# Four more query tiles in the paired front, differential heads spread over one more unit, and a conditioning block in the last projection of a two-layer diffusion trunk

## Chip, cores, metric

One core of a Trainium2 chip runs the whole program in one launch. The metric is device time in microseconds, the median over several executions. Engines are named as in the profile: PE is TensorE (PEld its weight loads), DVE VectorE, ACT ScalarE, POOL GpSimd, SP the sync engine that issues most DMAs.

## What is computed

512 latent tokens and 128 context tokens, 640 columns in all, of width 2048 pass two layers: a norm with shift and scale from a condition vector, one combined input projection, mixers with gates, an output projection, and a gated residual. Layer 1, which the change is about, in the reference's words (cut):

```python
def odd_mixer(h, w_in, w_out, cqn, ckn, c_lam, c_on, dqn, dkn, lam_init, ctx=None, rope=None):
    cq, ck, cv, cg, dq, dk, dv, dg = split_cols(h @ w_in, ODD_SPLIT)
...
    o1 = attend(cq[:, 0][:, :, None], ck_all[:, 0], cv_all)[:, :, 0]
    o2 = attend(cq[:, 1][:, :, None], ck_all[:, 1], cv_all)[:, :, 0]
    o_c = rms_norm(o1 - lam.astype(o1.dtype) * o2, c_on) * (1.0 - lam_init)
    y_c = o_c.transpose(0, 2, 1, 3).reshape(b, t, C_W) * jax.nn.silu(cg)
    y_d = merge_heads(attend(q_d, dk_all, dv_all)) * jax.nn.silu(dg)
    return jnp.concatenate([y_c, y_d], axis=-1) @ w_out, new
```

Mixer C has four differential heads, each with two softmax maps over the same values, so each needs two query tiles (cq h and cq 4 + h). Mixer D has eight ordinary heads, handled as four pairs that share a softmax step. Latent queries read 256 cached context keys and 512 latent keys; context queries read 128.

The shift, scale and gate come from a product of the condition with a 2048 x 6144 matrix for each layer, cut into twelve conditioning blocks of 512 columns. Block 11 of layer 1 holds the last quarter of the gate, needed for output columns 12 to 15 of the last projection.

## The kernel before, in words

Everything is float32, with operands split into a high and a low part (split, L336: ScalarE writes the high part, VectorE the low one), and each product made of three matmuls (high x high, low x high, high x low). Columns are the 640 tokens, in two halves of 320. A projected tile is 128 output columns for all tokens.

There are two ways to project. run_tiles (L430) makes a tile directly, over 16 input blocks, quarter by quarter; its weight quarters are loaded five and split three ahead. run_pairs (L583) makes two tiles at once with a Winograd form of Strassen's scheme: products M1, M5, M6, M2, M7, M3, M4, each over eight input blocks and one half of the tokens, from sums of weights and of inputs that VectorE forms. Between half products it calls slot (L421), which moves the waiting work on: late softmax scalings, prep (generators for keys, queries, values), attn (the attention generators, paced in steps per slot), and a fill generator, by a credit per product that rests gives.

Layer 1 runs in three stages.

*Front* (L1736 to L1863): six gate tiles directly, then 16 pairs: gates, ten keys, four queries of mixer D, ten values. Their results go to DRAM scratch (gdram, kdram, qdram, vdram). Keys are normed, turned and transposed back by key_chain (L1765). The fill, fill1, is ada_in_psum (L222) for blocks 8 to 10: weights of a block come in 16 loads on POOL's queue, and VectorE adds each, times two scalars, onto rows in PSUM; ada_fold (L257) then sums over partitions with matmuls and transposes back.

*Attention* (L1865 to L1968): 14 tiles by run_tiles: the four first queries of each pair of mixer D, then two queries for each head of mixer C, then two gates. After a query tile, q_gen (L791) or, for one that comes back from DRAM, q_rider (L813) norms and turns it; head_rest (L1924) brings keys and values. The attention work goes between the matmuls of the tiles: 3.1 steps per quarter for the first five tiles, 1.75 after. pair_gen (L953) and diff_gen (L1645) go through five blocks of 128 queries, one unit each, in two steps: score, softmax, transposes of the probabilities (groups), the product with the values (weigh), for differential heads the norm and the transposed output (out), each some units behind the score. Block 11 is made here, by ada_in_rows (L244), on VectorE with loads on SP's queue; its remaining calls run before the first pair of heads is set going (first, L1914).

*Last projection* (project_out, L1352, through project, L1309): two lead tiles whose inputs come in as the last head ends, four single tiles beside which forms (L1249) makes the sums of inputs, then five pairs, with rows transposed and stored.

PSUM tiles: one bank pair S for scores (two of them in the attention stage), two banks T for everything transposed or weighted. Tiles of the SBUF name "xr" rotate through five places. The order of instructions on an engine is that of the program as a list scheduler has laid it out, so an instruction with operands not ready yet can stand behind later ones.

## Time and profile before

| | us |
|---|---|
| median of 3 runs | 2247.62 (2247.52 to 2248.9) |
| the profiled execution | 2246.84 |
| its span, first to last instruction | 2245.1 |
| six gate tiles and 16 front pairs of layer 1 end | 1598.8 |
| attention stage | 1598.8 to 2018.5 |
| last projection | 2018.5 to 2241 |

Times in the trace count from the first instruction. A row of the busy view has a stretch, its length, then busy time and instructions of PE, PEld, DVE, ACT and POOL, the granted TensorE clock, the DMA engines' share and GB/s. A row of a group has line, engine, operation, output and inputs, count, then busy time, mean ns of one, and the idle time ahead of them with what ended it. A wait row has who waited for whom, total us, times, and the longest. A matmul's shown length overlaps the next one's, so matmuls are counted by their number in a stretch.

### The profile page before, as it was taken

The numbers are of one execution on the slowest core, as the hardware profiler recorded it, in microseconds if no ns is written. First come the engines' busy times: TensorE is split into PE (matmuls) and PEld (weight loads), VectorE is DVE, ScalarE is ACT, GpSimd is POOL, SyncE is SP. The second block draws the span as 40 slices with busy tenths as digits, with TensorE's granted clock in tenths as the row PEclk, the third lists the DMA queues.
The fourth block names the chain that finished last, engine by engine and source line by source line (L and its number), as shares of the span: only waits on it lengthen the run. The fifth ranks groups of instructions, "written<-read, shape, count | busy, mean of one in ns | idle before, by whom it ended". The sixth has DMA issues, their size and how long they took to land.

```text
span 2245.1 us, 41142 instructions
## 1 busy us (share of the span) xinstructions
PE 2202.9 (98%) x15516; PEld 2126.6 (95%) x15516; DVE 1748.3 (78%) x3047; ACT 1135.5 (51%) x2443; POOL 253.3 (11%) x405
## 2 busy tenths in 40 slices
PE   7999999999999999999999999999989999999999
PEld 5889999999999999999999999999978999999999
DVE  5659898989888977878788878887686567776665
ACT  4334453535344445444654466545567766664343
POOL 3221001000100100000101012211101001111010
PEclk9999999999999999999999999999999999999999
DMA  9985556565454435844774434545542233357541
GB/s 355 339 289 176 164 167 209 174 200 167 141 158 121 145 103 180 244 141 123 231 235 150 146 99 126 162 134 159 179 148 84 69 98 109 92 163 238 170 132 45
DMA packets 381399, 368.47 MB, mean 164 GB/s; under 512 B 18946, under 2 KB 326624, under 8 KB 380688
## 3 DMA queue, kind: packets, MB, share of 16 engines
q1 hardware_dynamic: 359552, 288.97, 43.0%
q0 software_dynamic: 20784, 74.63, 9.4%
q8 instruction: 122, 2.00, 0.4%
q10 hardware_dynamic: 864, 2.23, 0.3%
q14 instruction: 77, 0.63, 0.1%
HBM read 312.41 MB, written 48.11 MB: 161 GB/s over the span
## 4 chain that ended last, share of the span: by engine, by line
PE 84%; DVE 4%; DMA 4%; issue 4%; ACT 3%; POOL 1%; SPq 0%; DVEq 0%; POOLq 0%; ACTq 0%
PE pq L676 12%; PE pq L677 12%; PE pq L678 12%; PE pa L373 5%; PE pa L374 5%; PE pa L375 5%; PE pb L375 5%; PE pb L373 5%; PE pb L374 5%; PE T L914 2%; PE S L926 2%; PE S L928 1%; PE S L927 1%; PE T L196 1%; PE T L706 1%
## 5 line engine op out<-in xcount | busy, mean ns | idle before, releaser
L337 ACT ACTIVATE wh<-raw 128x512 fp32r<-128x512 f32 (+1 forms) x352 | 210.7, 600 | 324.0 <-PE pb L374 198.7
L676 PE MATMUL pq<-h,wh 128*128 128x320 f32 x1152 | 358.0, 311 | 0.0
L677 PE MATMUL pq<-h,wh 128*128 128x320 f32 x1152 | 356.0, 309 | 0.0
L678 PE MATMUL pq<-h,wl 128*128 128x320 f32 x1152 | 355.7, 309 | 0.0
L373 PE MATMUL pa<-h,wh 128*128 128x320 f32 x944 | 300.1, 318 | 0.0
L375 PE MATMUL pa<-h,wl 128*128 128x320 f32 x944 | 293.5, 311 | 3.3 <-DVE wl L338 3.3
L373 PE MATMUL pb<-h,wh 128*128 128x320 f32 x944 | 295.6, 314 | 1.1 <-ACT h L337 0.9
L375 PE MATMUL pb<-h,wl 128*128 128x320 f32 x944 | 294.5, 312 | 1.0 <-DVE wl L338 1.0
L374 PE MATMUL pa<-h,wh 128*128 128x320 f32 x944 | 294.5, 312 | 0.4 <-DVE h L338 0.4
L374 PE MATMUL pb<-h,wh 128*128 128x320 f32 x944 | 293.7, 311 | 0.0
L338 DVE TENSOR_TENSOR wl<-raw,wh 128x512 fp32r<-128x512 f32 (+1 forms) x352 | 228.5, 650 | 81.1 <-ACT wh L337 75.4
L676 PE MATMUL pq<-T,wh 128*128 128x320 f32 x864 | 268.7, 311 | 0.0
L678 PE MATMUL pq<-T,wl 128*128 128x320 f32 x864 | 267.2, 309 | 0.3 <-DVE wl L338 0.3
L677 PE MATMUL pq<-T,wh 128*128 128x320 f32 x864 | 266.9, 309 | 0.0
L337 ACT ACTIVATE wh<-sx 128x512 fp32r<-128x512 f32 x216 | 135.9, 632 | 171.5 <-PE pq L677 114.0
L676 PEld LDWEIGHTS pq<-h,wh 128*128 128x128 f32 x1152 | 216.3, 188 | 1.2 <-issue 1.2
L677 PEld LDWEIGHTS pq<-h,wh 128*128 128x128 f32 x1152 | 216.4, 188 | 0.0
L678 PEld LDWEIGHTS pq<-h,wl 128*128 128x128 f32 x1152 | 216.3, 188 | 0.0
L291 DVE SCALAR_TENSOR_TENSOR acc<-adaw,sT,acc 128x1024 f32<-128x1024 f32 x150 | 189.5, 1277 | 0.0
L373 PEld LDWEIGHTS pa<-h,wh 128*128 128x128 f32 x944 | 177.7, 188 | 10.2 <-issue 9.3
L374 PEld LDWEIGHTS pa<-h,wh 128*128 128x128 f32 x944 | 177.7, 188 | 5.2 <-issue 4.5
L375 PEld LDWEIGHTS pa<-h,wl 128*128 128x128 f32 x944 | 177.6, 188 | 4.4 <-DVE wl L338 3.6
(416 smaller groups left out, 5007.5 us busy)
## 6 DMA issues: line engine op xcount, KB each, us to landing
adaw<-in_ada_w SPq DMA_DIRECT2D x80, 512.0 KB, 4.2
raw<-in_ev_w_in SPq DMA_DIRECT2D x130, 256.0 KB, 3.5
raw<-in_od_w_in SPq DMA_DIRECT2D x112, 256.0 KB, 3.4
w<-in_od_w_in SPq DMA_DIRECT2D x48, 512.0 KB, 4.2
ada<-in_ada_w SPq DMA_DIRECT2D x11, 2048.0 KB, 13.5
adaw<-in_ada_w POOLq DMA_DIRECT2D x59, 256.0 KB, 3.5
w<-in_ev_w_in SPq DMA_DIRECT2D x27, 512.0 KB, 3.8
adah<-in_ada_w SPq DMA_DIRECT2D x20, 512.0 KB, 9.2
```

Of the source, the lines that this page charges most:

```text
L196: PE.matmul(acc[32 * g:32 * g + 32, 0:wd], sT[:, kt, :], w[:, kt % m, :], start=(i < 4), stop=(i >= KT - 4), tile_position=(0, 32 * g))
L291: V.scalar_tensor_tensor(out=acc[c], in0=w, scalar=sT[:, kt, c:c + 1], in1=acc[c], op0=ALU.mult, op1=ALU.add)
L337: A.activation(hi, x, AF.Copy)
L338: V.tensor_sub(lo, x, hi)
L373: PE.matmul(ps, wh[:, i, :], hi[:, sl], start=(j == js[0] if alone else (pos == 0 and j == 0)), stop=False)
L374: PE.matmul(ps, wh[:, i, :], lo[:, sl], start=False, stop=False)
L375: PE.matmul(ps, wl[:, i, :], hi[:, sl], start=False, stop=(j == js[1] - 1 if alone else (pos == 3 and j == 3)))
L676: PE.matmul(ps, wh[:, j, :], hi, start=(first and h == 0 and j == 0), stop=False, skip_group_check=True)
L677: PE.matmul(ps, wh[:, j, :], lo, start=False, stop=False, skip_group_check=True)
L678: PE.matmul(ps, wl[:, j, :], hi, start=False, stop=(final and h == 1 and j == 3), skip_group_check=True)
L914: PE.transpose(t[:, i * P:(i + 1) * P], p, ident)
L926: PE.matmul(d, q[0][:, bs], k[0][:, ks], start=True, stop=False)
```

## The change

Queries 4 to 7 of mixer C join the front's pairs and come back through q_rider, so that the attention stage has ten tiles. Its steps per quarter become 3.3 and 3.9. Attention generators start a step later, and a differential head's norm and output are spread over one more unit. In the product with the values the low halves come last. The square of a head's output writes PSUM in place of an SBUF tile. Block 11 becomes a fill of the last projection, from its fourth tile on, one load at a time on POOL's queue, with an end before the fourth pair; ada_fold becomes a generator with a pause between its steps. Keys get one more pause, and the fill rates of the front change. The two late gates wait for three finished heads.

```diff
-    def ada_in_psum(blocks):
+    def ada_in_psum(blocks, pool, place, n, tag, bufs):
...
-            fetch = lambda kt: ada_in(xr_tile("adaw")[:, 0:512], l, cb, kt, nc.gpsimd)
-            ws = [fetch(0), fetch(1)]
+            fetch = lambda kt: ada_in(place()[:, 0:512], l, cb, kt, nc.gpsimd)
+            ws = [fetch(kt) for kt in range(n)]
             yield
             for kt in range(KT):
                 for _ in ada_rows(l, cb, kt, ws[0], acc):
                     yield
                 ws.pop(0)
-                if kt + 2 < KT:
-                    ws.append(fetch(kt + 2))
...
+                if kt + n < KT:
+                    ws.append(fetch(kt + n))
+            yield from ada_folds(l, cb, acc, pools["cur"], tag, bufs, place)
             yield
...
-            for c0 in cs:
-                for i in range(c0, min(c0 + 2, len(chunks))):
-                    c, js, pt = chunks[i], slice((i - c0) * 256, (i - c0) * 256 + 256), pts[u, c0]
-                    PE.matmul(os[u], v[0][:, c, :], pt[0][:, js], start=(i == 0), stop=False)
-                    PE.matmul(os[u], v[0][:, c, :], pt[1][:, js], start=False, stop=False)
-                    PE.matmul(os[u], v[1][:, c, :], pt[0][:, js], start=False, stop=(i == len(chunks) - 1))
+            todo = [(i, chunks[i], slice((i - c0) * 256, (i - c0) * 256 + 256), pts[u, c0])
+                    for c0 in cs for i in range(c0, min(c0 + 2, len(chunks)))]
+            for i, c, js, pt in todo:
+                PE.matmul(os[u], v[0][:, c, :], pt[0][:, js], start=(i == 0), stop=False)
+                PE.matmul(os[u], v[1][:, c, :], pt[0][:, js], start=False, stop=False)
+            for i, c, js, pt in todo:
+                PE.matmul(os[u], v[0][:, c, :], pt[1][:, js], start=False, stop=(i == len(chunks) - 1))
...
+        if not banded:
+            yield
         for u in range(7):
...
+    place1 = lambda: xr_tile("adaw")
+    fill1 = ada_in_psum([(1, cb) for cb in range(8, 11)], lambda: pS, place1, 2, "xr", 5)
+    fill2 = ada_in_psum([(1, 11)], lambda: pS, place1, 1, "xr", 5)
...
                     advance(attn, 1 if len(hv) == 2 else 2)
+                    if n >= fill_at:
+                        next(fill, None)
                     go_on()
...
         def begin(p):
+            if n0 + 2 * p >= 12:
+                for _ in kw.get("fill") or ():
+                    pass
...
-            junk = ap.tile([P, 256], BF16, tag="junk", name="junk")
-            A.activation(junk, on, AF.Square, accum_out=ssq)
+            A.activation(o, on, AF.Square, accum_out=ssq)
...
-        for u in range(8):
-            if u >= 3:
-                out(u - 3)
+        yield
+        for u in range(9):
+            if u >= 4:
+                out(u - 4)
...
-            if u == 7:
+            if u == 8:
                 break
             yield
-            if u >= 2:
+            if 2 <= u < 7:
                 norm(u - 2)
...
         key_turn(kg, m1, xr_tile("m2")[:, 0:NS].rearrange("p (b f) -> p b f", b=4), sinF)
+        yield
         yield
...
-    FRONT_COLS += [OD["dq"] + i * P for i in (1, 3, 5, 7)]
-    FRONT_OUT += [(query_out, j) for j in range(4)]
+    FRONT_COLS += [OD["dq"] + i * P for i in (1, 3, 5, 7)] + [OD["cq"] + i * P for i in (4, 5, 6, 7)]
+    FRONT_OUT += [(query_out, j) for j in range(8)]
...
-            return {"M6": 0.5, "M2": 0.5, "M4": 1.0}.get(name, 0.0)
-        return {"M6": 1.0, "M2": 1.0, "M3": 1.0, "M4": 0.5 if out is gate_out else 1.25}.get(name, 0.0)
+            return {"M6": 0.5, "M2": 0.5, "M4": 0.5}.get(name, 0.0)
+        return {"M6": 1.0, "M2": 1.0, "M3": 1.0, "M4": 0.25 if out is gate_out else 1.25}.get(name, 0.0)
...
-    fill1 = ada_in_rows(1, 11)
...
-        def first():
-            for _ in fill1:
-                pass
-            return then()
-        rider = q_rider(n, "q1", (gains["d_q_norm"], vec[:, 157:158]), first)
+        rider = q_rider(n, "q1", (gains["d_q_norm"], vec[:, 158:159]), then)
...
     def head_rest(h, n):
         ap = pools["cur"]
+        rider = q_rider(4 + h, "q1", (gains["c_q_norm"], vec[:, 157:158]))
+        next(rider)
         k = key_load(2 + 2 * h, "kk", 2)
         yield
         yield
+        next(rider)
+        yield
+        next(rider, None)
         wait_for("scores", n)
...
-    for h in range(4):
-        jobs.append((OD["cq"] + h * P, q_job("q0", "c_q_norm")))
-        jobs.append((OD["cq"] + (4 + h) * P, with_rest("q1", "c_q_norm", head_rest, h, done0 + 4 + h)))
-    for i in (4, 5):
-        jobs.append((OD["cg"] + i * P, very_late_gate(i, (("rp", 3), ("stg", 2), ("rp", 3)))))
-    run_tiles(jobs, I["od_w_in"][0], None, fill1, FILL1, steps=lambda i: 3.1 if i < 5 else 1.75,
+    jobs += [(OD["cq"] + h * P, with_rest("q0", "c_q_norm", head_rest, h, done0 + 4 + h)) for h in range(4)]
+    def last_gate(i):
+        late = very_late_gate(i, (("rp", 3), ("stg", 2), ("rp", 3)))
+
+        def f(pp):
+            wait_for("heads", 3)
+            return late(pp)
+        return f
+
+    jobs += [(OD["cg"] + i * P, last_gate(i)) for i in (4, 5)]
+    run_tiles(jobs, I["od_w_in"][0], None, steps=lambda i: 3.3 if i < 5 else 3.9,
               single=lambda i: 0 if i else 2)
...
-                lead_pp=(0, 2))
+                lead_pp=(0, 2), fill=fill2, fill_at=3, rests=lambda p, name: float(name in ("M6", "M2", "M3", "M4")))
```

63 lines of the change are left out of this document (29 added, 34 removed).

## The prediction

> **What bounds the kernel now.** I read the page first, for the engine that is never free, then the busy time by stretches, cut where the stages of layer 1 begin and end, and then what TensorE waits for in each.
>
> ```profile
> span 2245.1 us, 41142 instructions
> PE 2202.9 (98%) x15516; PEld 2126.6 (95%) x15516; DVE 1748.3 (78%) x3047; ACT 1135.5 (51%) x2443; POOL 253.3 (11%) x405
> ```
>
> ```profile
> core 0: us, PE busy (x) PEld busy (x) DVE busy (x) ACT busy (x) POOL busy (x), PEclk, DMA share, GB/s
> 1160.00:1300.00 140.00, 140.00 (x957) 140.00 (x956) 118.60 (x186) 64.88 (x121) 14.05 (x26) 1.00 0.53 158
> 1300.00:1440.00 140.00, 137.24 (x953) 134.19 (x952) 114.98 (x189) 93.07 (x278) 32.03 (x51) 1.00 0.39 122
> 1440.00:1598.80 158.80, 158.80 (x1099) 157.89 (x1097) 127.44 (x193) 81.76 (x163) 22.79 (x43) 1.00 0.46 147
> 1598.80:1640.00 41.20, 39.64 (x272) 36.99 (x272) 30.85 (x56) 16.79 (x39) 4.52 (x5) 1.00 0.78 243
> 1640.00:1700.00 60.00, 51.24 (x336) 44.36 (x335) 43.62 (x84) 41.49 (x90) 4.04 (x4) 0.97 0.36 109
> 1700.00:1768.60 68.60, 68.19 (x486) 62.21 (x485) 43.69 (x85) 54.48 (x121) 5.23 (x5) 1.00 0.24 71
> 1768.60:2018.50 249.90, 248.66 (x1774) 240.06 (x1773) 174.92 (x336) 165.15 (x399) 32.48 (x54) 1.00 0.37 111
> 2018.50:2066.00 47.50, 47.20 (x331) 46.90 (x330) 29.73 (x57) 20.38 (x44) 7.26 (x13) 1.00 0.70 230
> 2066.00:2184.00 118.00, 117.40 (x808) 116.54 (x807) 82.75 (x138) 48.69 (x90) 10.32 (x16) 1.00 0.55 165
> ```
>
> TensorE is busy nearly all the time, so a matmul that goes is time that goes, and a stall that goes is too. The front pairs (gates and keys to 1440, queries and values to 1598.8) lose 2.8 us of 140 in the key stretch and otherwise nothing. The attention stage runs from 1598.8 to 2018.5; its real hole is 1640 to 1700: TensorE is idle for 60.00 - 51.24 = 8.8 us there. From 1700 on it hardly idles, with ScalarE at 79% (54.48 of 68.60) in the dense heads, and VectorE at 70% (174.92 of 249.90) in the last dense steps and the four differential heads.
>
> **Term A, the two more pairs.** A projected tile is 16 inputs x 2 halves x 3 matmuls = 96 matmuls; a front pair makes two tiles with 7 products x 8 x 3 = 168. The row 1160 to 1300 is nothing but those: 140 us / 957 = 0.1463 us each. Four tiles go: 4 x 96 x 0.1463 = 56.2 us. Two pairs come: 2 x 168 x 0.1463 = 49.2 us. Net **-7.0 us** of TensorE. The new pairs' own loads, splits and copies are those of the query pairs that run in 1440 to 1598.8 with no idle time of TensorE and VectorE at 80%, so TensorE hides them; if that cover went, they'd cost the difference to the key stretch, 2.8 us in 140, or 1 us.
>
> **Term B, the conditioning block leaves the start of attention.** Its 32 rows stand among the first queries' work on VectorE, and its fold on TensorE and ScalarE; the first pair of heads is only set going after the block's last call (L1914).
>
> ```profile
> L214 DVE SCALAR_TENSOR_TENSOR adap<-adap,sT 128x512 f32<-128x512 f32 x30 | 21.0, 747 | 3.1 <-DMA adap<-in_ada_w 2.8
> ```
>
> Four views show what it does to others: the chain of work within 1598 to 1720, by line; TensorE's waits from 1598.8 to 2018.5; ScalarE's longest wait in 1640 to 1660; and two short stretches, the first with the clock after the longest stall.
>
> ```profile
> by line: issue 12.1%; DVE adap L214 6.9%; PE T L914 5.4%; DMA qsw<-qx 5.1%; PE S L926 4.8%; PE Sp L373 4.0%; PE Sp L375 3.9%; PE T L978 3.9%; PE Sp L374 3.9%; PE T L977 3.8%; PE S L928 3.6%; PE S L927 3.6%; PE T L979 3.0%; DMA adap<-in_ada_
> ```
>
> ```profile
> PE pa L375 <- DVE wl L338: 3.3, 1, 3.3
> PE S L926 <- ACT p L895: 2.4, 2, 1.3
> PE T L978 <- DVE ptl L338: 1.1, 2, 0.7
> PE T L1705 <- DVE ptl L338: 1.0, 3, 0.3
> ...
> PE T L977 <- DVE ptl L338: 0.6, 1, 0.6
> ```
>
> ```profile
> ACT ada_sb L265 <- PE T L262: 5.9, 1, 5.9
> ```
>
> ```profile
> 1648.00:1651.50 3.50, 3.50 (x15) 1.59 (x13) 2.45 (x5) 0.00 (x0) 0.00 (x0) 0.51 0.70 204
> ```
>
> ```profile
> 1660.00:1680.00 20.00, 16.64 (x115) 14.09 (x114) 15.29 (x31) 19.11 (x42) 0.00 (x0) 1.00 0.30 83
> ```
>
> TensorE waits 3.3 us for a weight split that stands behind block rows on VectorE; the granted clock then falls to 0.51 for 3.5 us (1.7 us of work); ScalarE stands for 5.9 us in front of the fold's copy, and the exponentials behind it are late; from 1660 to 1680 it works 19.1 of 20 us to catch up, and TensorE idles 3.4. On the chain the rows hold 6.9% of 122 us, 8.4 us. Bounds: nothing (the dense heads are held by ScalarE anyway) to 8.8 + 1.7 = 10.5 us. The two waits with a name are 3.3 + 1.7 = 5; I take **-5 us**, the hole's remainder staying. What is late next is the turned query (the DMA of qsw, 5.1% of that chain).
>
> **Term C, small waits.** In the key stretch TensorE waits for the turned keys and one fold:
>
> ```profile
> PE T L706 <- DVE sq L752: 1.7, 4, 0.5
> PE T L268 <- ACT ada_sb L265: 0.5, 1, 0.5
> PE T L706 <- DVE acc L752: 0.4, 1, 0.4
> ```
>
> The extra slot in the key chain and the slot between a fold's matmuls and its transposes take these: 2.6 us at most. Outputs a unit later and the low halves weighted last (L974, L1684) take at most the ptl waits above, 1.1 + 1.0 + 0.6 = 2.7 us. Together **-4 us** of 0 to -5.3.
>
> **Term D, denser heads.** Nothing of the attention itself goes, but four of its fourteen tiles do, so each step has less projection beside it. The heads' row loses 56.2 us of TensorE: 249.9 - 56.2 = 193.7. Of the other engines only the split of the 16 weight quarters goes:
>
> ```profile
> L338 DVE TENSOR_TENSOR wl<-raw,wh 128x512 fp32r<-128x512 f32 x57 | 39.1, 688 | 22.6 <-ACT wh L337 21.2 <-PE T L840 0.6 <-DMA y<-gd 0.5
> L337 ACT ACTIVATE wh<-raw 128x512 fp32r<-128x512 f32 x57 | 35.9, 630 | 29.7 <-PE pb L374 22.5 <-PE Sp L374 4.6 <-DMA raw<-in_od_w_in 2.6
> ...
> L802 DVE TENSOR_TENSOR qm<-qx,tables 128x512 f32<-128x512 f32 x12 | 8.2, 683 | 0.3 <-ACT qx L795 0.3
> ...
> L824 DVE SCALAR_TENSOR_TENSOR qm<-x,vec,tables 128x512 f32<-128x512 f32 x4 | 3.0, 741 | 0.0
> ```
>
> VectorE: 174.9 - 16 x 0.688 = 163.9 us, 85% of 193.7; ScalarE: 165.2 - 16 x 0.630 = 155.1, 80%. A query read back has the same five steps on VectorE as one from PSUM, two of them 741 for 683 ns: 4 x 2 x 0.06 = 0.5 us, in D's rounding; the queue SP gets four more loads of 320 KB, ahead of weight loads that are issued five quarters early. No row shows the heads at this density. The nearest are the dense heads after 1700 (ScalarE 79%, TensorE idle 0.4 of 68.6, 0.6%) and the hole itself (8.8 of 60, 15%): 1.2 us to 193.7 x 0.15 = 29 us. The first is nearer in cover (another engine near 80%, no block in its queue), yet there VectorE was at 64%: I take 3%, **+6 us**. The numbers of steps agree with the fewer tiles: per dense pair one call more, per head 15 becomes 18, in all 118 becomes 134, and the pace offers 3 x 13.4 + 9 x 8 = 112 before and 3 x 14.2 + 5 x 16.6 = 126 after, so 6 calls were left for the last projection's first tiles and 8 will be; six fit there, two are drained: +0.5 us.
>
> The square of the head's output now writes PSUM and holds its bank until it ends:
>
> ```profile
> L1693 ACT ACTIVATE junk<-on 128x256 bf16<-128x256 f32 x20 | 8.2, 411 | 0.4
> ```
>
> 20 x 0.411 = 8.2 us at the worst, if TensorE stood for the bank each time; nothing if it never does. With transposes a unit apart I take +0.5 us.
>
> **Term E, the block in the last projection.** 32 rows of 0.747 us, 24 us, come to the stretch 2066 to 2184 (three single tiles, three pairs), where VectorE has 118.0 - 82.8 = 35.2 us free: 91% afterwards. The row 1160 to 1300 has VectorE at 85% with the same rows and TensorE never idle. Bounds: 0 to the whole overload if the rows also wait for their loads (rival 3). I take **+1 us**. The rows' loads move from SP to POOL, behind the output DMAs that wait for ScalarE; nothing but the block itself is behind them there.
>
> The Trainium skill, "SBUF — State Buffer", section "SBUF: two separate sides", speaks against that move: a DMA issued from POOL cannot write its descriptors while VectorE holds the port that the two share. The row of the same loads in the front pairs shows it otherwise:
>
> ```profile
> L219 POOL DMA_DIRECT2D adaw<-in_ada_w x48: 536/541/550, 1173.2 to 1577.4; - x48
> ```
>
> From 536 to 550 ns over 48 issues, beside a VectorE at 80 to 85%: none was held up. By the page's 3100 ns for a blocked one, an estimate of 16 x 2.6 = 41 us would pass on POOL, which the sum would feel only if rows then come late; by the row nothing passes.
>
> **Sum.** -7.0 - 5 - 4 + 6 + 0.5 + 0.5 + 1 = -8.0 us against the profiled execution, which took 2246.84 us for a span of 2245.1, so 2238.8. The median of the three timed runs is 2247.62, 0.8 above it: 2239.6, rounded **2239 us**. What a measurement of this kernel can tell from no change is about 0.2%, 4.5 us: faster is below 2243.1.
>
> **Rivals.**
>
> *1. More goes than I count (chance 0.13).* The whole hole closes and the heads run like 1700 to 1768: -7.0 - 10.5 - 5.3 + 1.2 + 1 = -20.6, **2227 us**. For it: attention could start its exponentials 5.9 us earlier, and the hole comes right after. Against it: ScalarE at 19.1 of 20 us may be the dense pairs' own load, and they are paced a little faster than before (3.3 for 3.1).
>
> *2. The density takes back what the pairs give (0.16).* The hole is ScalarE's own and stays but for half of B, and the heads lose 5%: -7.0 - 2.5 - 4 + 9.7 + 2 = -1.8, **2246 us**, no change. For it: VectorE at 85% with the maximum, the split and the mix of a unit in one queue.
>
> *3. Slower: the block's loads have one place and are late (0.06).* With one tile fetched at a time, a row's load is issued in the same call as its first use.
>
> ```profile
> adaw<-in_ada_w POOLq DMA_DIRECT2D x59, 256.0 KB, 3.5
> ```
>
> Landing takes 3.5 us, issue 0.54; calls are half a product apart (12 x 0.146 = 1.8 us), so VectorE would stand 16 x 2.2 = 36 us, of which 35.2 - 24 = 11 us are free: +25, **2264 us**. It decides from about 1.2 us of wait per load on. Against it: five tiles rotate behind the one name, so POOL can issue ahead.
>
> *4. Slower: the heads become bound by the chain through VectorE (0.12).* One score tile's maximum, exponential, transpose and split must end before TensorE gets its bank back. With one group of six projection matmuls between two steps (0.9 us; 3.9 / 4 steps per group) and not two or three (1.75 / 4), TensorE reaches the bank first. At the hole's rate it costs 29 us for my 6: **2262 us**; from 14 us (7%) on the change gains nothing.
>
> My forecast has 0.53, with 2232 to 2244 as its own range. Faster: 0.53 + 0.13 = 0.66. Same: rival 2, 0.16. Slower: rivals 3 and 4, 0.18. The range reaches from rival 1 to beyond no change, **2227 to 2255**; above it lie most of 3 and 4, below it half of 1.
>
> **What would show it.** 18 pairs ahead of attention, and that stage some 56 us shorter less its new idle time; no block row between 1599 and 1700 and no clock of 0.51 there; no wait of L706 for the turned keys; heads with VectorE near 85% and TensorE's idle time in them 5 to 8 us (rival 2: 10, rival 4: over 14); in the last projection, block rows with VectorE idle for their loads under 10 us. I am wrong if VectorE's loads in the last projection end TensorE's waits, or if weighting waits for the split in each unit.

## The result, and the profile after

| | before | after |
|---|---|---|
| median of 9 executions each | 2247.5 us | 2253.97 us |
| lowest to highest | 2242.65 to 2251.01 | 2251.68 to 2257.71 |
| profiled execution, its span | 2246.84, 2245.1 | 2251.68, 2249.9 |

The ratio is 1.0036, 95% interval 1.0026 to 1.0046: the change makes the kernel slower where 8 us faster was forecast. The ratio on record makes it 8 us, the two medians 6.5. The time is inside the range on record, on the other side of no change. The traces show one execution each, and the one after is the fastest of its nine. The page of the kernel after has 48 matmuls fewer, and 1.9 us less of busy TensorE in a span that is 4.8 us longer:

```profile
span 2249.9 us, 41154 instructions
...
PE 2201.0 (98%) x15468; PEld 2119.8 (94%) x15468; DVE 1766.5 (79%) x3075; ACT 1148.6 (51%) x2459; POOL 267.7 (12%) x429
```

The busy time by stretches (columns as in the prediction; the front pairs now end at 1643.1 and the attention stage at 2014.4, and the rows are cut as before, the same distances from the start of the stage):

```profile
core 0: us, PE busy (x) PEld busy (x) DVE busy (x) ACT busy (x) POOL busy (x), PEclk, DMA share, GB/s
...
1300.00:1440.00 140.00, 139.73 (x980) 138.64 (x979) 114.37 (x190) 93.72 (x282) 32.97 (x52) 1.00 0.40 123
1440.00:1643.10 203.10, 203.10 (x1400) 201.18 (x1399) 158.53 (x239) 102.03 (x198) 25.16 (x48) 1.00 0.45 139
1643.10:1684.00 40.90, 40.64 (x277) 38.65 (x276) 23.46 (x43) 23.83 (x54) 5.02 (x5) 1.00 0.72 225
1684.00:1744.00 60.00, 60.00 (x432) 54.98 (x431) 41.16 (x78) 48.63 (x105) 5.48 (x5) 1.00 0.21 65
1744.00:1812.00 68.00, 67.30 (x474) 62.65 (x474) 45.98 (x87) 51.47 (x115) 6.23 (x7) 1.00 0.36 109
1812.00:2014.40 202.40, 189.37 (x1312) 173.17 (x1311) 151.72 (x307) 144.71 (x358) 33.04 (x57) 0.99 0.34 106
2014.40:2066.00 51.60, 48.24 (x325) 46.93 (x324) 36.86 (x65) 19.34 (x31) 7.04 (x12) 1.00 0.79 253
2066.00:2184.00 118.00, 112.37 (x762) 110.09 (x761) 89.77 (x149) 47.42 (x90) 16.34 (x27) 0.99 0.57 176
```

Read stage by stage, TensorE's idle time has moved. The key stretch lost 2.8 us before and loses 0.3 now. The hole of 8.8 us in 1640 to 1700 is gone: its counterpart, 1684 to 1744, is full. But the heads' row idles 202.40 - 189.37 = 13.0 us, where before it was 1.2 of 249.9, and the last projection to 2184 idles 3.4 + 5.6 = 9.0 us, where it was 0.9. In stage lengths: front, from the start of its first matmul to that of its last, 463.6 us for 416.6 (+47.0), attention 371.3 for 419.7 (-48.4), from there to the end 235.5 for 226.6 (+8.9).

What TensorE waits for from 1840 to the end of the heads, and then in the last projection (waiter, releaser, total us, times, longest):

```profile
PE S L923 <- ACT p L892: 2.6, 1, 2.6
PE T L1712 <- DVE k0l L335: 1.4, 1, 1.4
PE T L1712 <- DVE on L1707: 1.4, 2, 0.8
PE S L923 <- ACT k1h L334: 1.3, 2, 0.9
PE T L1712 <- DVE ptl L335: 1.2, 3, 0.6
PE pa L370 <- ACT qsq L793: 1.1, 3, 0.7
```

```profile
PE T L703 <- DVE xr L1296: 6.4, 5, 2.6
PE T L703 <- issue: 2.2, 1, 2.2
```

In the heads no one row leads: score banks (S), transposes' banks (T) and keys all come late by a little. (The longest single wait, 2.6 us, is for a score bank that ScalarE's exponential still reads.) In the last projection one does: the transposes of finished rows (L703) wait for VectorE's residual sums (xr, L1296). After the long waits the granted clock halves, in these two stretches of 3.4 us among others:

```profile
1976.60:1980.00 3.40, 3.40 (x14) 3.40 (x13) 2.45 (x6) 1.61 (x4) 0.00 (x0) 0.50 0.69 214
2068.70:2072.10 3.40, 3.31 (x13) 2.94 (x14) 3.40 (x7) 2.18 (x4) 1.16 (x2) 0.51 0.62 207
```

### The profile page after: what moved, and what is told of

Same layout as the page of the kernel before. It is cut to its first block, busy times and chain, and to the rows that moved or that the text cites. A ratio compares the mean times of both kernels' runs of the same rounds, so it can differ in the third digit from the quotient of the medians.

```text
span 2249.9 us, 41154 instructions
## 1 busy us (share of the span) xinstructions
PE 2201.0 (98%) x15468; PEld 2119.8 (94%) x15468; DVE 1766.5 (79%) x3075; ACT 1148.6 (51%) x2459; POOL 267.7 (12%) x429
## 5 line engine op out<-in xcount | busy, mean ns | idle before, releaser
L673 PE MATMUL pq<-h,wh 128*128 128x320 f32 x1216 | 378.2, 311 | 0.0
L674 PE MATMUL pq<-h,wh 128*128 128x320 f32 x1216 | 375.7, 309 | 0.0
L675 PE MATMUL pq<-h,wl 128*128 128x320 f32 x1216 | 375.5, 309 | 0.0
L673 PE MATMUL pq<-T,wh 128*128 128x320 f32 x912 | 283.9, 311 | 0.3 <-DVE tables L652 0.3
L674 PE MATMUL pq<-T,wh 128*128 128x320 f32 x912 | 281.8, 309 | 0.0
L370 PE MATMUL pa<-h,wh 128*128 128x320 f32 x880 | 280.5, 319 | 1.1 <-ACT qsq L793 1.1
L370 PE MATMUL pb<-h,wh 128*128 128x320 f32 x880 | 276.6, 315 | 0.9 <-ACT h L334 0.9
L371 PE MATMUL pa<-h,wh 128*128 128x320 f32 x880 | 275.8, 313 | 1.0 <-DVE h L335 1.0
L372 PE MATMUL pb<-h,wl 128*128 128x320 f32 x880 | 274.3, 312 | 0.0
L371 PE MATMUL pb<-h,wh 128*128 128x320 f32 x880 | 273.1, 310 | 0.0
L673 PEld LDWEIGHTS pq<-h,wh 128*128 128x128 f32 x1216 | 228.4, 188 | 2.1 <-issue 2.1
L674 PEld LDWEIGHTS pq<-h,wh 128*128 128x128 f32 x1216 | 228.5, 188 | 0.0
L335 DVE TENSOR_TENSOR wl<-sx,wh 128x512 fp32r<-128x512 f32 x228 | 156.1, 689 | 46.8 <-ACT wh L334 40.9
L370 PEld LDWEIGHTS pa<-h,wh 128*128 128x128 f32 x880 | 166.4, 189 | 12.9 <-issue 9.7
L673 PEld LDWEIGHTS pq<-T,wh 128*128 128x128 f32 x912 | 171.5, 188 | 1.0 <-issue 0.9
## 6 DMA issues: line engine op xcount, KB each, us to landing
ada<-in_ada_w SPq DMA_DIRECT2D x11, 2048.0 KB, 13.5
```

The lines of the kernel that those rows point to most:

```text
L335: V.tensor_sub(lo, x, hi)
L370: PE.matmul(ps, wh[:, i, :], hi[:, sl], start=(j == js[0] if alone else (pos == 0 and j == 0)), stop=False)
L371: PE.matmul(ps, wh[:, i, :], lo[:, sl], start=False, stop=False)
L372: PE.matmul(ps, wl[:, i, :], hi[:, sl], start=False, stop=(j == js[1] - 1 if alone else (pos == 3 and j == 3)))
L673: PE.matmul(ps, wh[:, j, :], hi, start=(first and h == 0 and j == 0), stop=False, skip_group_check=True)
L674: PE.matmul(ps, wh[:, j, :], lo, start=False, stop=False, skip_group_check=True)
```

## The experiments

Two theories at first. **H**: the heads lose it, because the pairs took away the projection matmuls beside them. **L**: the last projection loses it, because of block 11. Later ones split H into the steps' pace, VectorE's rate, the T banks and the distance between dependent steps. All kernels were timed beside the kernel before, on several chips, so the ratios are compared and not the times. The table puts them in an order in which neighbours mostly differ by one edit (e8, g1 and f4 also hold the scaling edit of e5, which the scheduler all but undid; the kernels with block 11 in the front have higher fill rates there). The other runs stand in the text only. "Forced" is how many of the attention's steps wait_for runs at a stroke, with no projection call between them, counted in the program.

| kernel | tiles in attention | block 11 | steps a call, forced | ratio to before (95%) |
|---|---|---|---|---|
| before | 14 | heads' start | 1.75, 0 | 1 |
| h1_before_block_last | 14 | last projection | 1.75, 0 | 0.9960 (0.9948 to 0.9972) |
| e3_before_block_in_front | 14 | front | 1.75, 0 | 0.9937 (0.9925 to 0.9950) |
| g4_14_tiles_block_last, with the small edits from here on | 14 | last projection | 2.0, 0 | 0.9949 (0.9934 to 0.9963) |
| f2_14_tiles_in_time | 14 | front | 2.0, 0 | 0.9951 (0.9938 to 0.9963) |
| g2_14_tiles_slow_steps | 14 | front | 1.75, 7 | 0.9974 (0.9965 to 0.9982) |
| g1_12_tiles_in_time | 12 | front | 4.2, 0 | 0.9961 (0.9948 to 0.9974) |
| f4_12_tiles | 12 | front | 3.0, 9 | 0.9994 (0.9986 to 1.0003) |
| e8_scale_later_pace | 10 | front | 4.5, 0 | 0.9966 (0.9953 to 0.9979) |
| e1_block_in_front | 10 | front | 3.9, 4 | 1.0003 (0.9995 to 1.0012) |
| e4_pace | 10 | last projection | 4.5, 0 | 1.0011 (1.0002 to 1.0020) |
| after | 10 | last projection | 3.9, 4 | 1.0036 (1.0026 to 1.0046) |

### Where block 11 goes: e1, e2, e3

e1, on the kernel after (cut: its fill rates in the front go up too, by M7 and M5, so that the fourth block gets done); e3 is the same on the kernel before, without ada_in_rows:

```diff
-    fill1 = ada_in_psum([(1, cb) for cb in range(8, 11)], lambda: pS, place1, 2, "xr", 5)
-    fill2 = ada_in_psum([(1, 11)], lambda: pS, place1, 1, "xr", 5)
+    fill1 = ada_in_psum([(1, cb) for cb in range(8, 12)], lambda: pS, place1, 2, "xr", 5)
...
-                lead_pp=(0, 2), fill=fill2, fill_at=3, rests=lambda p, name: float(name in ("M6", "M2", "M3", "M4")))
+                lead_pp=(0, 2))
```

e2, on the kernel after (and three places for the residual rows, not five):

```diff
+    place2 = lambda: pools["cur"].tile([P, 512], F32, tag="fw", name="adaw", bufs=2)
-    fill2 = ada_in_psum([(1, 11)], lambda: pS, place1, 1, "xr", 5)
+    fill2 = ada_in_psum([(1, 11)], lambda: pS, place2, 1, "fw", 2)
```

> The changed kernel with block 11 made as a fourth fill block in the front pairs and nothing of it in the last projection. Theory L (the block in the last projection costs what the trace shows there, 92.3 -> 97.0 us for tiles and 128.9 -> 133.1 us for pairs): those stretches go back to about 92 and 129, and the time falls by 8 to 9 us, to about 2245. Theory H (all of the loss lies in the heads, the last projection only shows waits that would be elsewhere): within 2 us of the changed kernel, 2252 to 2256. If VectorE in the front becomes the bound at some 90%, idle time of TensorE appears there and eats part of it.

> The changed kernel with two places of their own for the block's loads in the last projection, and three for the residual tiles in place of five shared. If the shared rotation is the cause (residual loads on SP's queue wait for block rows, and the inputs behind them come late): the 5.5 us and 4.4 us that VectorE waits for inputs go, and 6 to 8 us of the 9 come back, about 2247. If VectorE's load alone is the cause: no more than 2 us, 2252 to 2256.

> The kernel before with its fourteen tiles, block 11 made in the front pairs in place of the start of attention; nothing else. If the hole at 1640 to 1700 is the block's: TensorE's 8.8 us of idle time and 1.7 us of half clock go, 8 to 11 us faster than before, about 2238. If it is ScalarE's own load from the dense heads: 2 to 5 us, about 2244.

e1: 2249.55 us, ratio 1.0003, 0.33% (7.4 us) under the change: L holds for that share, and only for that share. e3: 2235.44 us, ratio 0.9937, so the block's place at the start of the heads cost the kernel before more than the forecast gave it. e2: 2253.05 us, 1.0021: its time is in the range for VectorE's load alone, its ratio some 3 us under the change, with intervals that overlap. e1's waits in the last projection against the change's: the wait for the residual sums is all but gone.

```profile
PE T L703 <- issue: 1.8, 2, 1.2
PE T L703 <- DVE xr L1295: 0.7, 2, 0.5
```

Yet e1 and e3, both with the block in the front, are 0.66% apart: there H begins.

### The pace: e4

```diff
-    run_tiles(jobs, I["od_w_in"][0], None, steps=lambda i: 3.3 if i < 5 else 3.9,
+    run_tiles(jobs, I["od_w_in"][0], None, steps=lambda i: 3.3 if i < 5 else 4.5,
```

> The changed kernel with 4.5 steps per quarter for the tiles from the sixth on, in place of 3.9, so that 19 and not 16.6 calls of the attention generators go beside each tile (a head has 18). If the idle time in the heads comes from steps that are forced with no projection beside them (wait_for at the head's values and at the gates): the burst around 1970 goes, TensorE's idle time in the heads falls from 13 to about 6 us, and the time by 6 to 8 us, to about 2247. If it comes from the density itself: within 2 us, or slower by up to 4 as steps bunch more.

2252.96 us, 1.0011: 0.25% (5.6 us) under the change, nearly what was expected of forced steps. The fall of the idle time to 6 us doesn't show in the trace: the same stretch of the heads (1817.1 to 2019.5) idles 12.9 us in the profiled execution, which is the slowest of the eleven. With 3.9 the program forces two steps before the last head's keys and two before the first gate; with 4.5 none. e1 has the same pace as the change and shows such a place. From 1976 to 1987.9 no matmul of a tile runs between the attention's own; in it stand one long wait, two of 0.5 and 0.6 us ahead of it, and the clock behind them:

```profile
PE S L923 <- ACT p L892: 2.6, 1, 2.6
```

```profile
1984.80:1988.20 3.40, 3.00 (x10) 3.00 (x11) 1.79 (x5) 1.61 (x5) 0.00 (x0) 0.50 0.76 230
```

### VectorE's wait for the norm, and the first undoing of the pairs: e5 to e8

In e1's heads VectorE stands behind GpSimd's power (rn), with key splits queued behind it (VectorE's waits in e1's heads, then in e5's):

```profile
DVE on L1706 <- POOL rn L1702: 15.8, 16, 3.8
```

```profile
DVE on L1706 <- POOL rn L1702: 13.8, 14, 3.8
```

e5, on e1 (e7 is the same edit on e6, e8 on e1 with 4.5 steps):

```diff
             if u >= 4:
                 out(u - 4)
+            if 3 <= u < 8:
+                norm(u - 3)
...
-            if 2 <= u < 7:
-                norm(u - 2)
```

e6, on e1: the two pairs undone.

```diff
-    FRONT_COLS += [OD["dq"] + i * P for i in (1, 3, 5, 7)] + [OD["cq"] + i * P for i in (4, 5, 6, 7)]
+    FRONT_COLS += [OD["dq"] + i * P for i in (1, 3, 5, 7)]
...
-    jobs += [(OD["cq"] + h * P, with_rest("q0", "c_q_norm", head_rest, h, done0 + 4 + h)) for h in range(4)]
+    for h in range(4):
+        jobs.append((OD["cq"] + h * P, q_job("q0", "c_q_norm")))
+        jobs.append((OD["cq"] + (4 + h) * P, with_rest("q1", "c_q_norm", head_rest, h, done0 + 4 + h)))
```

> The kernel after with block 11 in the front (measured beside before: 2249.6 to 2249.5) and one more edit: VectorE's scaling of a head's output rows is issued half a unit later, ahead of the next unit's weighing, and no more in the half unit of its own weighing. In that kernel's heads VectorE stood 15.8 us in 16 waits for the row's power on GpSimd (7.5 us in 11 before the change), longest 3.8 us, with key and probability splits queued behind, and TensorE stood idle 13 us. Theory V (VectorE held in order behind that wait is what the denser heads lose by): those waits fall under 6 us, TensorE's idle time by 6 to 9 us, and the time to about 2241 (2239 to 2244). Rival R (each step's whole chain is too long for the few projection matmuls left, wherever VectorE waits): the waits move to other rows, time 2248 to 2251.

> The two pairs alone undone: the kernel after with block 11 in the front, all eight context queries as tiles of their own beside the heads again (14 tiles, step pace 2.0), the small edits kept (low halves last, outputs a unit later, the longer key pause, the square into PSUM). If the density that the pairs bring is where the time went: 2231 to 2237, near the kernel before with block 11 in the front (2235.4). If the small edits lose it: 2247 to 2257, since the pairs' own gain of 7.0 us is given up too.

> The 14 tiles as in the run above and VectorE's scaling half a unit later. Theory V: with the projection matmuls of 14 tiles as cover the wait is hidden anyway (TensorE idle under 2 us in those heads), so within 2 us of the run above. Rival: if VectorE's stand also costs where TensorE is covered, 4 us or more below it.

> The scaling half a unit later and 4.5 steps a call in place of 3.9 from the sixth tile on. If the forced steps ahead of the first gate are a loss of their own (a stand of 2.6 us and a half-clock stretch of 3.4 us there): 2 to 5 us below the run with the scaling alone. If the pace only moves the idle time about: within 2 us of it.

e5: 2248.75 us, 0.9999, as rival R has it. But the wait hardly moved: the scheduler put the scaling back nearly where it was, so theory V (VectorE's place in line behind that wait is what the denser heads lose by) was not put to the test. In e7 VectorE's order came out nearly the same as in e6, and so the two (2251.6 and 2250.37 us, 1.0008 and 1.0003) show how closely one order repeats: 0.05%.

e6's 2251.6 us lies in the range for small edits that lose the time, but its trace gives another reason. With two front pairs fewer, block 11 was not done in time; its fold was drained at the stage's end, where TensorE stood 13.5 us, to 1613.8, and then ran at half clock to 1619.5 (the wait, then two stretches: the slow one, which begins within the stand, and the heads):

```profile
PE T L258 <- ACT adaw L248: 13.5, 1, 13.5
```

```profile
1602.40:1619.50 17.10, 5.73 (x24) 4.58 (x25) 6.54 (x13) 2.08 (x4) 1.01 (x2) 0.50 0.48 178
1770.00:2018.00 248.00, 247.09 (x1755) 238.66 (x1754) 173.28 (x332) 166.23 (x398) 31.29 (x53) 1.00 0.37 112
```

The heads themselves idle 0.9 us of 248. So the 14 tiles do cover them, and f2 is the same with the block in time. e8: 2241.72 us, 0.9966, 0.33% under e5, with the pace its only other edit: the forced steps are a loss of their own, 7.4 us where 2 to 5 were expected; TensorE's idle time in the heads falls from 12.4 to 9.8 us.

### What the denser heads wait for: f1 to f4

f1, on e8 (st["last_s"] is the latest score tile, of which columns 0 to 127 and 896 to 1023 are free):

```diff
-            A.activation(o, on, AF.Square, accum_out=ssq)
+            spare = st["last_s"].rearrange("p (a b) -> p a b", b=P)[:, 0:8:7, :]
+            A.activation(spare, on.rearrange("p (a b) -> p a b", b=P), AF.Square, accum_out=ssq)
```

f2, on e6; f3, on e8; f4, on e8, with two tiles put back beside the heads and their pair taken out of the front (17 front pairs; cut, M5 is 0.5 here too):

```diff
-            return {"M6": 0.5, "M2": 0.5, "M4": 0.5, "M7": 0.75, "M5": 0.25}.get(name, 0.0)
-        return {"M6": 1.0, "M2": 1.0, "M3": 1.0, "M4": 0.25 if out is gate_out else 1.25, "M7": 0.75, "M5": 0.25}.get(name, 0.0)
+            return {"M6": 0.5, "M2": 0.5, "M4": 1.0, "M7": 0.75, "M5": 0.5}.get(name, 0.0)
+        return {"M6": 1.0, "M2": 1.0, "M3": 1.0, "M4": 0.5 if out is gate_out else 1.25, "M7": 0.75, "M5": 0.5}.get(name, 0.0)
```

```diff
                 groups(u - 1)
+            for _ in range(2):
+                V.tensor_scalar(st["con"], st["con"], 1.0, None, ALU.mult)
             yield
```

```diff
-    FRONT_COLS += [OD["dq"] + i * P for i in (1, 3, 5, 7)] + [OD["cq"] + i * P for i in (4, 5, 6, 7)]
+    FRONT_COLS += [OD["dq"] + i * P for i in (1, 3, 5, 7)] + [OD["cq"] + i * P for i in (6, 7)]
...
-    run_tiles(jobs, I["od_w_in"][0], None, steps=lambda i: 3.3 if i < 5 else 4.5,
+    run_tiles(jobs, I["od_w_in"][0], None, steps=lambda i: 3.3 if i < 5 else 3.0,
```

> The kernel with block 11 in the front, 4.5 steps a call and the scaling half a unit later (2241.7 beside before at 2248.6), and one more edit: the square of a head's output rows is written into the free columns of the latest score tile and no more into the T place that holds them. If the two T places are what the denser heads wait for (waits of TensorE for a place that VectorE or ScalarE still reads were 5 us of that run's heads): 20 holds shorter by 0.4 us each, TensorE's idle time in the heads 2 to 5 us less, 2237 to 2240. If the places are not what binds: 2240.5 to 2244.

> The two pairs alone undone, as in the earlier run, whose block 11 was not done with two front pairs fewer and stood at the stage's end (13.5 us of TensorE's time, half clock for 17.1 us); here the block's and the pairs' rests are those of the kernel before with block 11 in the front, so that it is done in time. Its heads stood no more than in the kernel before in that earlier run. If the density that the pairs bring is where the time went and the small edits cost nothing: 2230 to 2236, that is 13 to 19 us below the same kernel with the pairs at 2249.6. If the small edits lose by themselves: 2240 or more.

> The 4.5-step kernel (2241.7) with VectorE's load raised in the heads: 72 more multiplications by one of the 256-column table of the norm, some 0.3 to 0.5 us each, 20 to 35 us in all, that nothing but later scalings reads. VectorE is busy some 77% of the heads there. If VectorE's rate binds the denser heads: 8 to 25 us slower, 2250 to 2267. If what binds is the chain from one engine to the next and VectorE's idle time takes the additions: under 4 us, 2241 to 2246.

> Half of the pairs' density: the 4.5-step kernel with the second queries of heads 6 and 7 in the front and those of heads 4 and 5 as tiles beside the heads (12 tiles, 18 pairs, 3.0 steps a call). If the loss grows evenly with each tile that goes: midway between 14 tiles (about 2234) and 10 (2241.7), 2237 to 2239. If there is a point from which it sets in (a tile gone costs nothing while TensorE still has cover): 2230 to 2235, with TensorE's idle time in the first two heads as with 14 tiles and in the last two as with 10.

f2: 2235.7 us, 0.9951, as H expects: 0.52% under e1 and, by the intervals, level with e3 (0.14% apart), so the small edits cost nothing that can be told from noise beside 14 tiles. The heads of f2, e8 and f3, one row each:

```profile
1768.00:2010.00 242.00, 239.90 (x1708) 231.59 (x1707) 170.37 (x331) 162.25 (x393) 32.87 (x54) 1.00 0.37 113
```

```profile
1814.00:2014.90 200.90, 191.13 (x1342) 175.81 (x1342) 152.19 (x313) 148.28 (x369) 32.78 (x57) 1.00 0.36 109
```

```profile
1812.00:2011.50 199.50, 191.30 (x1346) 176.46 (x1345) 165.19 (x371) 149.16 (x369) 34.29 (x57) 1.00 0.36 111
```

```profile
L1740 DVE TENSOR_SCALAR con<-con 128x256 f32<-128x256 f32 x56 | 15.9, 284 | 0.3
```

TensorE idles 2.1 us with 14 tiles and 9.8 with 10. f3 gives VectorE 15.9 us more to do in that window (less than was expected); VectorE is busy 83% of it for e8's 76%, and TensorE idles 8.2 us, no more than in e8. The time is 2238.19 us, 0.9964, level with e8. So VectorE's rate does not bind the denser heads, up to that load. f1: 2244.95 us, 0.9991, above both expectations and 0.25% above e8: no gain, and TensorE idles 10.9 us of 204.3 in the heads, so the square's hold of a T bank is not what they lose by. Why it is slower than e8 the profile doesn't say (its profiled execution is one of its faster ones, e8's the slowest of five).

What TensorE and VectorE wait for most in e8 from 1805 to 2024:

```profile
PE T L1711 <- DVE ptl L335: 3.4, 3, 1.5
DVE ptl L335 <- ACT pth L334: 16.2, 10, 2.7
```

With no forced steps one row does lead. A head's transposed outputs (L1711) wait for a T bank until VectorE has split probabilities (ptl), and VectorE waits for ScalarE's part of that split (pth); in the kernel before, VectorE's wait is 2.7 us in 3. Of the 8.2 us in e8's seven longest rows of TensorE's waits VectorE ends 6.7. That is a chain from engine to engine and not VectorE's rate. No run shortens that one chain, so its share is not shown.

f4 (2245.47 us, 0.9994) came out slower than 10 tiles, by neither theory; its program had nine forced steps, which the next run takes away.

### Pace or density, and the last two questions: g1 to g4, h1, h2

g1 is f4 with 4.2 for 3.0; g2 is f2 with 1.75 for 2.0; g4 is f2 with the block as in the change (the lines of e1 the other way round). h1 takes the small edits out of g4 as well, so that only the block's move, with the pause in its fold, is left of the change. h2 is e2 with 4.5 for 3.9. g3, on e8:

```diff
-        for u in range(9):
-            if u >= 4:
-                out(u - 4)
-            if 3 <= u < 8:
-                norm(u - 3)
+        for u in range(8):
+            if u >= 3:
+                out(u - 3)
...
             yield
+            if u >= 2:
+                norm(u - 2)
```

> The 12-tile kernel of the earlier run with 4.2 steps a call in place of 3.0. Counted in the program, 3.0 forced 9 steps of the heads at one place each without a projection tile's call between them (1, 1, 4, 1 and 2); 4.2 forces none. If forced steps are a price of their own: 5 to 9 us below that run's 0.9994 of the kernel before, a ratio of 0.995 to 0.997, and between 14 tiles (0.9951) and 10 tiles (0.9966). If the density alone set that time: 0.9985 to 1.0005.

> The 14-tile kernel (0.9951 of before) with 1.75 steps a call in place of 2.0, by which 7 steps are forced (1 and 2 of them behind the third head, 2 ahead of the first gate, 2 at the end). If forced steps cost by themselves, even where 14 tiles cover the heads: 3 to 7 us more, a ratio of 0.9965 to 0.998. If they cost only in the denser heads: within 2 us, 0.9942 to 0.996.

> The 10-tile kernel with 4.5 steps a call (0.9966 of before) with the head's outputs and scalings in the units of the kernel before: outputs three units behind their scores and no more four, so that a head's tail is a unit shorter. If the longer tail, with few matmuls in it, is what the heads' boundaries lose by: 2 to 5 us less, 0.9943 to 0.9957. If the later outputs spare TensorE waits, as was meant: 3 to 8 us more, 0.998 to 1.0002.

> The 14-tile kernel with block 11 taken out of the front and put beside the last projection's lone tiles, as in the kernel after: the two pairs alone undone from the change. If the block in the last projection costs by itself what it cost beside the denser heads (0.33%, after to the same with the block in the front): 0.9975 to 0.999. If that price came of what the denser heads left late: 0.9945 to 0.9965.

> One part of the change alone: the kernel before, its 14 tiles and its heads, with block 11 beside the last projection's lone tiles as in the kernel after. If the block's move gains by itself what its move to the front gained (0.9937): 0.993 to 0.996, 2232 to 2239. If in the last projection it costs what it cost beside the denser heads: 0.997 or more.

> The kernel after with both mends: 4.5 steps a call (alone 1.0011 of before) and two places of their own for the block's loads (alone 1.0021). With block 11 in the front the same pace gave 0.9966. If the shared places are most of the block's price beside the denser heads: 0.9965 to 0.9985. If they are a small part: 0.9995 to 1.001.

g1: 2241.44 us, 0.9961, and g2: 2243.39 us, 0.9974: forced steps cost by themselves, 0.33% for nine and 0.23% for seven, even beside 14 tiles. The heads of g2, f4 and g1:

```profile
1770.00:2018.00 248.00, 242.42 (x1703) 232.88 (x1703) 170.26 (x326) 163.84 (x394) 32.26 (x54) 0.99 0.37 112
```

```profile
1800.00:2014.00 214.00, 204.10 (x1411) 191.18 (x1409) 152.26 (x300) 141.53 (x353) 31.01 (x53) 0.98 0.36 110
```

```profile
1800.00:2011.00 211.00, 203.84 (x1433) 190.98 (x1432) 150.00 (x305) 143.64 (x356) 33.80 (x57) 1.00 0.36 108
```

TensorE idles 5.6 us in g2 for f2's 2.1, and 9.9 in f4 for g1's 7.2, with the clock under 1.00 in both. With no step forced the idle time falls in the order of the tiles: 9.8 us with 10, 7.2 with 12, 2.1 with 14 (in windows of 200.9, 211 and 242 us).

g3: 2249.87 us, 1.0006, 0.40% (9 us) above e8, a little more than expected; the idle time is 15.1 us:

```profile
1812.00:2016.00 204.00, 188.87 (x1315) 172.18 (x1314) 151.22 (x308) 144.32 (x359) 31.53 (x57) 1.00 0.35 106
```

So the later outputs spare waits in the denser heads, as they were meant to. VectorE has the same work in both (152.2 us in e8, 151.2 here), and ScalarE nearly (148.3 and 144.3): what helps is distance between dependent steps, not less work.

g4: 2238.91 us, 0.9949, by its time the case in which the price of the block comes of the denser heads; h1: 2240.4 us, 0.9960, at the edge of the expected gain. The block's move alone makes the kernel before 0.40% faster; in h1 the hole is closed (the stretches of the prediction's view, and the last projection):

```profile
1598.80:1640.00 41.20, 41.20 (x285) 39.14 (x278) 22.84 (x44) 23.50 (x54) 4.38 (x4) 1.00 0.70 217
1640.00:1700.00 60.00, 58.35 (x413) 53.69 (x413) 41.45 (x79) 47.70 (x102) 3.84 (x4) 1.00 0.22 67
1700.00:1768.60 68.60, 68.50 (x486) 63.15 (x485) 44.64 (x85) 51.89 (x114) 7.56 (x8) 1.00 0.30 92
2010.00:2184.00 174.00, 168.95 (x1154) 166.43 (x1153) 132.23 (x227) 69.62 (x129) 25.83 (x44) 0.99 0.62 193
```

and the last projection of e3, with the block in the front, and of g4:

```profile
2010.00:2184.00 174.00, 173.71 (x1206) 173.36 (x1205) 118.86 (x203) 72.45 (x135) 18.12 (x30) 1.00 0.58 180
```

```profile
2012.00:2184.00 172.00, 163.94 (x1111) 161.16 (x1110) 127.09 (x218) 65.74 (x121) 24.77 (x42) 0.98 0.61 192
```

There TensorE idles 5.1 us in h1 for 0.3 in e3, and 8.1 in g4 for 2.0 of 174.00 in f2. By time h1 is 0.23% above e3, with intervals that just touch. So the traces speak against the reading by g4's time alone: the price stands by itself, with 14 tiles as with 10. That g4 and f2 take the same time fits a price of the block in the front too, where there are two pairs fewer to hide it (f2's front pairs take 419.2 us, 1180.7 to 1599.9, g4's 412.3, 1182.0 to 1594.3). h2: 2250.96 us, 1.0003, 0.08% under e4, within what the intervals leave: the shared places are at most a small part.

## Why the prediction was wrong, by its terms

By the two profiled executions, stage by stage, where the forecast had -8.0. (Its 2239.6 us rounds to 2240, not 2239; nothing hangs on it.) That the time fell inside the range is luck: B gained 8 us more than forecast, and D and E lost 22 more.

**A, two more pairs, -7.0: right.** The front grew by 47.0 us, which is A's 49.2 less 2.2 that belong to C. The attention stage lost its 56.2 us of matmuls, as the count on the page and D below bear out.

**B, the block leaves the heads' start, -5, bounds 0 to -10.5: the mechanism right, the size beyond its bound.** In 1598.8 to 1768.6 the kernel before ran 272 + 336 + 486 = 1094 matmuls; h1 runs 285 + 413 + 486 = 1184 there. The 90 more are 90 x 0.1463 = 13.2 us, an estimate at a projection matmul's price. The same instruction in both traces says nearly the same: the first transposed output of a differential head starts 247.5 us after the front's end before (1846.3 - 1598.8), and 232.7 us in h1 (1831.7 - 1599.0), 14.8 us sooner; e3's time, 0.63% under before, agrees. I had counted idle time and half clock alone, 8.8 + 1.7 in the hole; the rest of the loss stands in no row as idle time.

**C, small waits, -4: half of it shown.** The key stretch idles 0.3 us in place of 2.8, and the front is 2.2 us shorter for it. The later outputs gain 9 us in the denser heads (g3), but the small edits together gain nothing that shows beside 14 tiles (g4 against h1, 0.11%, inside the intervals): the outputs pay back part of what D costs.

**D, denser heads, +6, pace +0.5, square +0.5: this is the step that failed.** The attention stage shrank by 48.4 us. With 56.2 for the four tiles and 13.2 for the hole it should have shrunk by 69.4, so the heads lost 69.4 - 48.4 = 21 us, a remainder: 3% was forecast, 11% of 193.7 came. It has two parts. The pace, +0.5 in the sum, is one: I counted steps left over for the next stage, not that wait_for runs the missing ones at a stroke. e4 against after, e8 against e5 and g1 against f4 put it at 0.25 to 0.33%, 5.6 to 7.4 us. The other, some 14 us, goes with the density itself. By times it is some 10: with no step forced in either, e8 with 10 tiles is 0.15% (3.4 us) above f2 with 14, though A takes 7.0 us from it. The runs exclude VectorE's rate (f3) and give no support to the square's hold (f1); idle time falls with more tiles (f2, g1) and with more distance between dependent steps (g3). Rival 4 had named the kind of thing, a chain through VectorE that keeps banks from TensorE, and its break-even of 14 us; nearly that much idle time came (13.0 us), and the half clock beside it. e8's waits point to such a chain, and no run tests it alone, so why fewer tiles leave TensorE waiting stays open beyond that. Of my "would show" list, VectorE at 85% did not come either: it is at 75% (151.72 of 202.40), because part of the 163.9 us forecast for the row ran ahead of it once the hole was closed, and because the heads took longer. "Weighting waits for the split in each unit", one of my signs of being wrong, did not come (0.9 us in 3 waits of L1693 from 1840 to 2014.4).

I took D from the dense heads after 1700 as the nearest row. That row has two heads in one step, a differential head goes alone, and the forecast had no row for that at this density.

**E, the block in the last projection, +1: mis-sized too.** That part of the kernel takes 8.9 us more, nearly all of it idle TensorE (9.0 for 0.9 to 2184). VectorE's waits there, in the kernel after:

```profile
DVE adaS L213 <- DMA adaw<-in_ada_w: 7.9, 5, 3.2
DVE tables L1279 <- DMA w<-yd: 5.5, 1, 5.5
DVE sf L1279 <- DMA w<-yd: 4.4, 2, 3.1
```

VectorE, 76% busy in 2066 to 2184 and not 91%, stands for the block's loads, as rival 3 had it, but 7.9 us in 5 waits, not 36 in 16, and for inputs of the forms that come late; the residual sums that TensorE waits for are behind in the same queue. The late inputs alone don't make the loss: e1, without the block here, has them too (4.8 and 2.4 us in the same two rows from 2022.9 to 2190, for 1.7 and 1.5 before), and there TensorE waits 0.7 us for the sums. So the sign that I had named, loads on VectorE that end TensorE's waits, came in part. As I read it, my comparison with the front, where the same rows stop nothing, missed that no such deadline stands behind them there. That the five shared places are the reason is not shown: places of their own gave 0.15% in one run and 0.08% in another, at the edge of the intervals. How the rest divides between late loads and the rows' own time stays open. The loads on POOL were not held up themselves:

```profile
L218 POOL DMA_DIRECT2D adaw<-in_ada_w x64: 538/543/552, 1169.5 to 2137.1; - x64
```

So the rule of the Trainium skill that the prediction weighed there ("SBUF — State Buffer", "SBUF: two separate sides") again shows no effect here.

**Sum.** -7.0 - 13.2 - 2.2 + 21 + 8.9 = +7.5 us; it closes by construction, as D's 21 is a remainder. The profiled executions differ by 4.8; the front pairs start 2.5 us earlier in the one after (1179.4 for 1181.9), ahead of anything that the change touches, and that is nearly all of the rest. The ratio on record says +8.1, the medians +6.5.

The fastest of these by its ratio is e3, level by the intervals with g4 and f2: of the whole change only the block's move out of the heads, and that into the front, 0.9937 of before. With 14 tiles the small edits change nothing to be seen. Two tiles that leave the heads save 3.5 us of matmuls, and even with no step forced nothing of it comes back (0.9951 with 14, 0.9961 with 12, 0.9966 with 10, by the intervals level or a little worse).

## What to carry to other kernels

Work that is moved out of a stage takes its cover along: before counting its saving, look at what the stage waits for when that work is not between its dependent steps, and buy distance between those steps first. When a stage gets fewer calls, recompute the pace of whatever is driven by those calls, and look for loops that run what is missing at a stroke. And try the parts of a change one by one: here one part gained 9 to 14 us and the others took it back.

## What the runs showed of the hardware

The granted clock halved here after stands shorter than the 3.3 us that I had reckoned with, and in stretches of one length or a multiple: 3.4 us in e1 (at 0.50), 6.8 in e4, 17.1 in e6, five times 3.4. No stand of 3.4 us is needed. Ahead of e1's slow stretch there was a wait of 2.6 us, with two of 0.5 and 0.6 before it; in the 3.4 us right ahead (1981.4 to 1984.8) TensorE was busy for 0.76. In the kernel after it was 0.83 us ahead of 1976.6 and 0.43 ahead of 2068.7, in the kernel before 1.50 us ahead of 1648.0.

The Trainium skill, "TensorE: Matmul & The Clock Gate", section "Part 1: The HAM clock gate (the "warmup" mystery)", has the clock decided over windows of about 3.4 us that run freely, and its table has it fall after at least one idle window. The lengths here agree; the stretches ahead were idle for the most part and not wholly.

A stretch of 3.4 us full of matmuls at a clock of 0.50 costs about 1.7 us beside the stand, an estimate; in the kernel after it held 14 matmuls (1976.6 to 1980.0), the next 3.4 us 24. What of it falls into the stand costs nothing more: in e6 that was 11.4 of the 17.1 us, from 1602.4 to 1613.8.
